# Another order of issue for the 3004 operations of a two-layer decoder trunk

## The chip, the cores and the metric

One core of one Trainium2 chip runs the whole kernel. The time is device microseconds (us) of one execution; the figure for the kernel is the median of its runs. The profile names the engines PE (TensorE, matmuls), PEld (its weight loads, which run beside it), DVE (VectorE), ACT (ScalarE), POOL (GpSimd) and SP (SyncE, which issues most DMA transfers).

## The reference

One sequence of 256 tokens with 1024 channels goes through two layers. Each layer normalises, scales and shifts the input by a vector that a small product with `w_ada` gives, mixes the tokens, and adds the gated result. The even layer has two attention branches (a sliding window with sinks, and a sparse one with compressed, selected and window keys), the odd layer one block-sparse branch with 16 heads of 64.

```python
for layer in range(DEPTH):
    ada = jnp.einsum('bd,de->be', c_act, w_ada[layer]) + b_ada[layer]
    shift, scale, gate = jnp.split(ada, 3, axis=-1)
    h = rms_norm(x, norm_g[layer]) * (1.0 + scale[:, None, :]) + shift[:, None, :]
    ...
    y = even_mixer(...) if layer % 2 == 0 else odd_mixer(h, w_in_odd[i], w_out_odd[i], cos, sin)
    x = x + gate[:, None, :] * y
return rms_norm(x, final_g)

def odd_mixer(h, w_in, w_out, cos, sin):
    proj = jnp.einsum('bsd,de->bse', h, w_in)
    q, k, v, z = jnp.split(proj, _offsets(ODD_SIZES), axis=-1)
    o = moba_attention(q, k, v, cos, sin) * jax.nn.silu(z)
    return jnp.einsum('bse,ed->bsd', o, w_out)
```

## The kernel before

The tokens are two halves of 128 partitions. Weights come in pieces of up to 1 MB into five buffers named `raw`. Full float32 precision is kept by splitting both operands into a high and a low part: ACT casts the high part (`whi`), DVE subtracts it for the low part (`wlo`), and each product is three matmuls, high by high, high by low and low by high (`mm3`; `split`, `load_split` and `split_quad` make the parts). For the activations the parts are called `hhi`, `hlo` and, after the gate path, `ghi`, `glo`. Products land in eight PSUM banks, named `ps_pj`, `ps_s`, `ps_pt`, `ps_o` and `ps_m` by their use.

The vector `ada` is made beside this: `ada_wide` loads pieces of `w_ada` and DVE adds them up, times the condition `cz`, in `acc`; then small matmuls sum `acc` over the partitions (`ada_shift_scale`, `start_sums`, `ada_gate`). The result that scales and shifts the input is `shs`.

Small f32 matmuls use a part of the array each, given by `tile_position`: strips of 32 or 64 rows or columns. `ada_shift_scale` has four column strips, `attn_quad` (attention scores of the odd layer) four row strips, `attn_four` and `attn_values` two strips. Each of these functions hands the list of its matmuls to `plan.group`, which gives all of them the same dependences, so that their order within the group is free but for sums that add up in one place.

What sets the order: the program is written with `Plan`, whose engines record each operation with its dependences in place of issuing it. At the end `issue` issues them all in the order of the list `ORDER` (3004 numbers from line 38 on; number n is the n-th operation recorded). Each engine works through its own instructions in that order, a DMA on the queue of the engine that issues it (nearly all on SP). The names of tiles and buffers were bound while recording, so a list can only reorder: what an operation reads, writes and waits for is fixed. Since every operation is issued by one line, the profile puts nearly all at line 249, and operations are told apart by the names of their tiles.

```python
def issue(self):
    place = {i: n for n, i in enumerate(ORDER)}
    assert len(place) == len(ORDER) == len(self.ops)
    for i in ORDER:
        assert all(place[d] < place[i] for d in self.ops[i]["deps"])
        self.ops[i]["inst"] = self.ops[i]["fn"]()
```

Of the kernel before, what the change touches and what calls it, by code (L numbers as in the profile page):

```python
# [37 lines left out]
0 2 1 4 5 44 9 685 3 10 6 37 88 11 7 38 35 12 87 13 89 14 15 16 86 17 18 85 19 70 90 20 91 21 71 22 92 55 72 23 93 47  # L38
45 24 41 56 25 48 74 57 26 49 94 73 27 28 40 59 58 80 95 42 29 75 50 30 76 104 60 61 62 51 63 77 78 98 65 64 66 67 106
107 108 109 110 111 112 113 114 115 116 52 117 101 79 118 119 120 121 122 123 124 125 126 127 128 129 53 105 130 131  # L40
132 133 134 135 136 137 96 68 97 138 81 145 139 82 31 69 140 83 32 141 100 33 142 147 34 146 99 182 170 149 164 148
183 151 171 143 150 173 84 179 167 102 165 144 158 185 152 186 176 153 103 177 159 178 156 172 154 174 212 200 201 157
213 160 180 184 155 168 162 206 222 36 187 224 194 166 531 175 225 169 195 181 215 188 226 203 189 207 223 202 227 214
228 229 230 231 232 233 234 235 236 161 237 238 239 240 241 242 243 220 244 245 163 246 247 190 248 197 191 198 208
249 204 217 192 257 196 250 209 251 216 259 252 205 199 258 210 274 261 211 253 286 260 283 255 275 295 254 289 530
268 287 262 193 256 277 219 276 290 218 264 296 292 272 288 221 270 284 273 280 269 281 322 266 293 285 334 263 294
324 282 271 278 291 323 297 335 279 307 313 319 267 325 308 314 310 332 301 265 302 336 316 326 304 303 333 337 338
339 340 341 342 343 344 345 346 347 348 349 329 350 351 352 353 354 355 356 357 305 358 320 309 306 311 327 365 312
359 298 367 317 366 328 299 315 330 360 318 361 321 368 362 300 433 363 371 384 369 436 390 402 364 385 393 370 403
405 529 378 391 437 399 396 373 386 331 372 397 374 394 435 380 379 398 420 387 382 438 432 400 376 401 406 404 381  # L50
423 434 388 407 439 389 421 534 408 392 383 411 440 528 395 429 409 687 414 375 424 441 425 430 377 442 443 444 445
446 447 448 449 450 451 452 453 417 454 415 426 455 418 412 413 456 463 422 457 532 459 410 458 416 533 431 464 427
465 682 480 467 419 466 461 492 489 501 460 478 495 481 469 483 468 486 470 476 484 479 502 683 462 482 474 485 428
490 684 471 491 496 475 507 472 497 513 8 504 477 503 505 506 473 493 498 540 499 541 514 932 555 508 509 686 525 557
487 556 519 809 515 537 526 527 558 538 488 500 543 535 494 510 539 607 520 551 516 511 608 542 553 559 517 552 521
536 518 512 554 545 522 549 560 550 546 565 609 566 544 561 934 562 563 617 564 610 571 931 567 572 568 569 690 616
936 573 629 619 620 621 933 611 622 523 570 630 623 577 612 578 574 575 576 618 524 579 583 580 613 581 688 584 585
586 582 638 589 590 631 624 614 632 637 633 625 591 592 626 634 671 627 587 593 689 588 628 595 596 597 598 635 599
600 640 547 641 636 639 642 643 594 548 601 602 644 603 658 604 605 606 659 650 645 646 664 647 651 648 665 652 653
649 654 660 692 655 691 693 694 661 657 662 695 696 656 697 698 663 699 700 666 810 701 702 935 703 670 704 667 668  # L60
705 672 706 707 669 708 938 709 1014 812 710 811 673 674 956 937 742 39 743 43 744 46 745 675 746 813 747 748 749 940
941 942 943 944 945 946 947 957 1021 756 959 960 961 962 963 964 965 966 939 1024 750 948 949 950 951 754 952 953 954
955 751 676 755 958 677 757 967 968 969 970 971 972 973 974 752 1131 678 753 1209 776 679 975 711 54 774 680 1212 712
778 713 714 758 780 715 782 976 759 977 775 978 760 761 979 681 762 716 768 980 864 865 866 779 867 981 868 615 982
874 869 870 781 871 983 872 777 990 984 985 878 986 987 717 783 896 718 880 719 989 764 763 784 720 902 721 722 723
875 988 724 876 725 991 785 1022 769 992 726 787 727 728 993 729 898 765 766 730 900 731 732 786 767 733 734 994 735
1023 1025 736 995 737 738 739 770 771 772 901 996 792 1330 1026 773 1079 1080 1081 740 1082 1083 1084 903 1085 1086
741 873 788 1091 789 793 790 997 814 815 816 791 817 818 1089 897 998 999 1000 1001 1132 1027 819 820 821 822 823 824
1002 825 1109 826 879 827 1133 1003 794 828 829 877 830 831 832 881 1004 795 796 882 833 1111 834 835 836 1005 837 838
839 1115 840 841 842 1093 843 1116 844 845 1087 846 883 847 899 1113 848 849 1006 850 851 885 852 1210 853 854 855 797  # L70
856 857 858 904 859 1090 860 861 1028 1134 905 1135 862 1136 1137 1138 891 1139 1140 906 1141 884 1215 1337 1007 863
798 799 1338 800 907 801 1211 802 909 803 804 1110 805 886 1114 887 888 890 1029 1030 1088 1008 1031 1032 1033 1142
889 1034 914 1035 1036 1331 915 1037 1038 892 893 1143 894 1039 1040 1041 895 1042 1043 908 1044 1009 1045 1332 1046
1047 1112 1048 1049 910 911 1094 1050 1051 1052 1053 1146 1054 1092 1055 1415 1117 912 1010 1056 1057 1058 806 913
1059 1060 1061 1213 1062 1333 1011 1095 1164 1012 1063 1216 1064 916 917 918 1065 1066 1067 1013 919 1068 1096 1334
1069 1070 807 1071 1072 1073 1074 1015 1075 1165 1335 1148 1098 1214 1016 1149 1076 1017 1018 1104 1019 1166 920 921
1020 1414 922 1144 923 1077 924 1168 1411 925 1170 926 1147 927 1410 1118 1078 1267 1145 1268 1269 1270 1097 1120 1339
1099 1126 1100 1101 1217 1218 1150 1171 1219 928 1220 1221 1222 1102 1223 1224 1151 1340 1225 1226 1167 1227 1228 1229
1230 1169 1231 1232 1233 1153 1234 1103 1235 1236 1416 808 1237 929 1238 1239 1240 1407 1241 1172 1105 1275 1242 1436
1243 1125 1406 1244 1245 1152 1246 1279 1247 1248 1119 1249 1250 1173 1158 1434 1106 1107 1437 1251 1252 1253 1254  # L80
1255 1256 1257 1108 1258 1259 1260 1281 1438 1261 1262 1263 1435 1264 1121 1122 1123 1265 1271 1272 1273 1274 1124
1266 1494 1159 1127 1128 1297 1417 1129 1181 1442 1299 1443 1130 1444 1301 1445 1277 1440 1154 1303 1155 1156 1180
1341 930 1342 1157 1343 1344 1175 1174 1441 1160 1161 1278 1162 1446 1447 1163 1454 1455 1280 1439 1176 1177 1298 1178
1456 1457 1179 1458 1459 1351 1276 1182 1504 1355 1183 1300 1184 1408 1345 1185 1346 1347 1348 1302 1186 1304 1187
1371 1188 1375 1189 1282 1353 1190 1373 1191 1192 1193 1349 1374 1194 1305 1283 1195 1306 1196 1284 1197 1409 1356
1198 1199 1352 1200 1201 1202 1286 1203 1285 1204 1431 1307 1292 1205 1412 1287 1314 1430 1288 1289 1448 1449 1354
1450 1350 1451 1206 1452 1308 1453 1460 1357 1290 1291 1461 1358 1413 1534 1462 1293 1294 1295 1463 1464 1296 1465
1535 1491 1566 1207 1542 1309 1490 1310 1311 1466 1313 1543 1377 1312 1544 1545 1359 1360 1418 1315 1316 1317 1467
1546 1318 1472 1567 1372 1336 1361 1362 1366 1363 1419 1319 1376 1320 1321 1378 1322 1323 1536 1324 1325 1379 1326
1365 1505 1380 1327 1208 1328 1495 1364 1420 1421 1422 1423 1329 1382 1381 1367 1432 1368 1424 1369 1547 1473 1370  # L90
1468 1387 1474 1433 1388 1383 1384 1385 1475 1476 1386 1469 1568 1492 1425 1389 1390 1391 1569 1548 1392 1470 1537
1393 1394 1395 1396 1397 1493 1398 1399 1400 1401 1402 1426 1403 1570 1652 1471 1549 1404 1477 1506 1550 1405 1507
1484 1538 1485 1478 1720 1486 1487 1488 1539 1489 1479 1480 1481 1482 1428 1500 1483 1571 1572 1501 1540 1551 1552
1553 1496 1554 1502 1555 1541 1556 1557 1656 1558 1559 1654 1560 1561 1781 1562 1655 1563 1564 1565 1497 1573 1574
1590 1575 1498 1576 1577 1427 1591 1578 1499 1579 1580 1581 1592 1582 1583 1584 1657 1596 1585 1586 1429 1587 1588
# [1272 lines left out]
```

## Time and profile before

| | |
|---|---|
| median of 3 runs | 298.74 us (298.65 to 298.84) |
| the profiled execution, first to last instruction | 296.8 us |
| granted TensorE clock, mean | 0.992 |
| moved by DMA | 71.73 MB, mean 242 GB/s |

The page's table of 40 slices shows what each engine does over the span, a digit for the busy tenths of 7.4 us:

```profile
DVE  0488698799999999999798679799959779999883
ACT  5356246876997899984638863286386338684531
DMA  7999999998992679686886969729828800192003
```

DMA engines are full for about the first 90 us, VectorE nearly full from 60 us on with some gaps, ScalarE and the later DMA half to three quarters used.

### The profile page before, as it was taken

To read this page: it belongs to the slowest core of one execution; us is meant where nothing else is said; L and a number is where in the kernel's file an instruction comes from. 1 tells how busy PE (TensorE), PEld (TensorE's weight loads), DVE (VectorE), ACT (ScalarE), POOL (GpSimd) and SP (SyncE) were. 2 spreads that over 40 slices of the span, in tenths; PEclk is the share of its full clock that TensorE was granted. 3 is DMA by queue.
4 is the path that set the end of the run, shared out by engine and by line. 5 is a ranking of instruction groups with operands and counts; after the bars stand their busy time and mean duration, and the time that the engine had idled before them with its cause. 6 is when DMAs were issued, how large, how long until landed. Compare 5 with 4: busy or idle time off the path is not lost.

```text
span 296.8 us, 6205 instructions
## 1 busy us (share of the span) xinstructions
PE 286.9 (97%) x2297; PEld 246.3 (83%) x2297; DVE 252.2 (85%) x630; ACT 188.5 (63%) x479; POOL 9.2 (3%) x32
## 2 busy tenths in 40 slices
PE   8999999999999999999999999999999989999991
PEld 8778778897788978776768899998899989887891
DVE  0488698799999999999798679799959779999883
ACT  5356246876997899984638863286386338684531
POOL 2100000001000000000020000000000000000021
PEclk9999999999999999999999999999999999999996
DMA  7999999998992679686886969729828800192003
GB/s 242 389 389 377 344 394 372 300 355 240 390 386 71 235 252 352 210 281 212 305 264 190 367 179 301 275 79 311 300 93 280 280 9 2 42 380 75 3 0 141
DMA packets 48479, 71.73 MB, mean 242 GB/s; under 512 B 2522, under 2 KB 33986, under 8 KB 48450
## 3 DMA queue, kind: packets, MB, share of 16 engines
q1 hardware_dynamic: 47906, 70.92, 70.0%
q10 hardware_dynamic: 544, 0.43, 0.4%
q8 instruction: 18, 0.29, 0.4%
q14 instruction: 11, 0.09, 0.1%
HBM read 70.29 MB, written 1.05 MB: 240 GB/s over the span
## 4 chain that ended last, share of the span: by engine, by line
PE 77%; DMA 14%; DVE 4%; ACT 2%; issue 1%; SPq 1%; POOL 1%; DVEq 0%; ACTq 0%
PE ps_pj L249 53%; PE ps_pt L249 7%; PE ps_o L249 6%; PE ps_s L249 6%; PE ps_m L249 5%; DMA raw<-in_w_in_even_dram 5%; DMA qT<-in_w_ada_dram 4%; DMA raw<-in_w_ada_dram 3%; DMA late<-in_w_ada_dram 2%; DVE wlo L249 1%; ACT whi L249 1%; SPq L249 1%; DVE xs L249 1%; DVE t L249 1%; POOL parts L249 1%
## 5 line engine op out<-in xcount | busy, mean ns | idle before, releaser
L249 ACT CAST whi<-raw 128x512 fp32r<-128x512 f32 (+2 forms) x116 | 72.2, 656 | 23.6 <-PE ps_pj L249 18.5
L249 DVE TENSOR_TENSOR wlo<-raw,whi 128x512 fp32r<-128x512 f32 (+2 forms) x100 | 71.8, 741 | 8.9 <-ACT whi L249 8.8
L249 PE MATMUL ps_pj<-hlo,whi 128*128 128x256 f32 x256 | 69.8, 286 | 0.0
L249 PE MATMUL ps_pj<-hhi,wlo 128*128 128x256 f32 x256 | 69.6, 284 | 0.0
L249 PE MATMUL ps_pj<-hhi,whi 128*128 128x256 f32 x256 | 69.5, 286 | 0.0
L249 PEld LDWEIGHTS ps_pj<-hhi,wlo 128*128 128x128 f32 x256 | 47.4, 188 | 1.7 <-issue 1.3
L249 PEld LDWEIGHTS ps_pj<-hhi,whi 128*128 128x128 f32 x256 | 47.0, 188 | 1.1 <-issue 0.3
L249 PEld LDWEIGHTS ps_pj<-hlo,whi 128*128 128x128 f32 x256 | 47.1, 188 | 0.5 <-issue 0.2
L249 DVE SCALAR_TENSOR_TENSOR acc<-raw,cz,acc 128x1024 f32<-128x1024 f32 x24 | 30.7, 1278 | 2.1 <-DMA raw<-in_w_ada_dram 2.0
L249 ACT ACTIVATE late<-late,mn 128x128 f32<-128x128 f32 (+1 forms) x58 | 25.9, 448 | 8.4 <-DVE mn L249 8.4
L249 DVE SCALAR_TENSOR_TENSOR wlo<-raw,whi 128x512 fp32r<-128x512 f32 x32 | 21.4, 686 | 6.3 <-ACT whi L249 6.2
L249 PE MATMUL ps_pj<-whi,hhi 128*128 128x512 f32 (+2 forms) x72 | 25.7, 376 | 0.6 <-ACT hhi L249 0.5
L249 PE MATMUL ps_pj<-whi,hlo 128*128 128x512 f32 (+2 forms) x72 | 26.0, 372 | 0.0
L249 PE MATMUL ps_pj<-wlo,hhi 128*128 128x512 f32 (+2 forms) x72 | 25.6, 367 | 0.0
L249 ACT COPY late<-ps_pt 128x384 f32<-128x384 f32 (+1 forms) x29 | 14.0, 484 | 12.9 <-PE ps_pt L249 12.9
L249 PE MATMUL ps_pj<-whi,ghi 128*128 128x512 f32 (+1 forms) x56 | 20.8, 372 | 0.0
L249 PE MATMUL ps_pj<-wlo,ghi 128*128 128x512 f32 (+1 forms) x56 | 20.5, 366 | 0.0
L249 PE MATMUL ps_pj<-whi,glo 128*128 128x512 f32 (+1 forms) x56 | 20.4, 366 | 0.0
L249 PE MATMUL ps_pt<-ta,late 128*128 128x128 f32 x87 | 16.5, 278 | 0.9 <-DVE late L249 0.9
L249 PEld LDWEIGHTS ps_pj<-whi,hhi 128*128 128x128 f32 x72 | 13.5, 188 | 3.2 <-ACT hhi L249 1.2
L249 ACT ACTIVATE whi<-raw 128x512 fp32r<-128x512 f32 x16 | 10.0, 629 | 9.0 <-PE ps_pj L249 8.7
L249 PEld LDWEIGHTS ps_pj<-whi,hlo 128*128 128x128 f32 x72 | 13.5, 188 | 1.8 <-issue 0.2
(240 smaller groups left out, 589.6 us busy)
## 6 DMA issues: line engine op xcount, KB each, us to landing
raw<-in_w_in_odd_dram SPq DMA_DIRECT2D x16, 1024.0 KB, 5.8
raw<-in_w_ada_dram SPq DMA_DIRECT2D x8, 1024.0 KB, 7.8
raw<-in_w_ada_dram SPq DMA_DIRECT2D x16, 512.0 KB, 6.0
raw<-in_w_in_even_dram SPq DMA_DIRECT2D x5, 1024.0 KB, 9.0
raw<-in_w_in_even_dram SPq DMA_DIRECT2D x7, 652.0 KB, 6.7
late<-in_w_ada_dram SPq DMA_DIRECT2D x16, 256.0 KB, 6.6
raw<-in_w_out_even_dram SPq DMA_DIRECT2D x4, 1024.0 KB, 5.4
raw<-in_w_out_odd_dram SPq DMA_DIRECT2D x4, 1024.0 KB, 9.2
```

The costliest lines, as they stand in the source:

```text
L249: self.ops.append(dict(key=eng.key, deps=deps, fn=lambda: getattr(real, name)(*args, **kw)))
```

## The change

`ORDER` gets another list of the same 3004 numbers. Nothing else differs: operations, tiles, dependences and transfers stay, and each operation stays on its engine. The diff is a block of numbers:

```diff
@@ -35,127 +35,123 @@
-0 2 1 4 5 44 9 685 3 10 6 37 88 11 7 38 35 12 87 13 89 14 15 16 86 17 18 85 19 70 90 20 91 21 71 22 92 55 72 23 93 47
...
-1503 1598 1597 1589 1599 1658 1600 1601 1593 1602 1611 1508 1509 1510 1511 1512 1513 1514 1515 1603 1516 1517 1518
...
+1581 1592 1582 1502 1583 1584 1657 1596 1658 1585 1586 1503 1587 1597 1598 1588 1655 1589 1599 1600 1601 1593 1602 1508
...
```

By engine, the operations that stand at another place in their queue are 1339 of 1912 on PE, 453 of 546 on DVE, 313 of 397 on ACT, 78 of 121 on SP and 17 of 28 on POOL. The first some 10 us and PE's last part, from about 269 us on, keep their order. (The lines of the list are four fewer, so that line 249 is line 245 in the new file.)

Three places show what that means. The rows are an engine's operations in the order of issue: line, operation, output <- inputs with the buffers' numbers, and shape; "x2" means twice in a row.

**The start, DVE at about 36 us.** `raw4` is a piece of `w_in_even`, `wlo` its low part; `shs` is the shift and scale of four channel groups; `oT` and then `hhi`, `hlo` (ACT, DVE) are the scaled input. Before:

```order
L249 SCALAR_TENSOR_TENSOR acc0_106<-qT1_99,cz_72,acc0_106 128x512 x2
L249 TENSOR_TENSOR wlo0_114<-raw4_105,whi0_110 128x512
L249 TENSOR_TENSOR shs_76<-ps_m0_107,rT_73 128x2x2
L249 TENSOR_TENSOR shs_76<-shs_76,rT_73 128x2
L249 TENSOR_TENSOR wlo0_114<-raw4_105,whi0_110 128x512
L249 TENSOR_SCALAR oT_74<-bigA_84,shs_76 128x256
```

and now:

```order
L245 SCALAR_TENSOR_TENSOR acc0_106<-qT1_99,cz_72,acc0_106 128x512
L245 TENSOR_TENSOR shs_76<-ps_m0_107,rT_73 128x2x2
L245 TENSOR_TENSOR shs_76<-shs_76,rT_73 128x2
L245 TENSOR_SCALAR oT_74<-bigA_84,shs_76 128x256
L245 TENSOR_TENSOR wlo0_114<-raw4_105,whi0_110 128x512
L245 TENSOR_SCALAR oT_74<-bigA_84,shs_76 128x256
```

Both splits of `raw4` moved behind `shs`.

**The last load of `w_ada`, SP at about 230 us.** It goes to `raw2`, the last piece but one of the odd layer's input weights to `raw1`. Before:

```order
L249 DMA raw0_101<-in_w_in_odd_dram 128x8x256
L249 DMA raw3_104<-in_w_out_odd_dram 128x4x512
L249 DMA raw1_102<-in_w_in_odd_dram 128x8x256
L249 DMA raw2_103<-in_w_ada_dram 128x2x1024
L249 DMA raw1_102<-in_w_out_odd_dram 128x4x512
```

and now:

```order
L245 DMA raw0_101<-in_w_in_odd_dram 128x8x256
L245 DMA raw3_104<-in_w_out_odd_dram 128x4x512
L245 DMA raw2_103<-in_w_ada_dram 128x2x1024
L245 DMA raw1_102<-in_w_in_odd_dram 128x8x256
L245 DMA gate_77<-in_b_ada_dram 128x1024
```

The two loads changed places. On DVE the product `late_81<-late_81,rc41_149 128x128` that a transpose at 243 us waits for moved from behind the accumulation `acc0_106<-raw2_103,cz_72,acc0_106` to 14 places further ahead.

**A packed group, PE at about 153.6 us.** These are the matmuls of `ada_shift_scale` for the odd layer: five sums of 128 terms on each of four column strips. Before:

```order
L249 MATMUL ps_pj2_96<-ta_63,t40_88 128x128 x4
L249 MATMUL ps_o0_68<-ta_63,t40_88 128x128
L249 MATMUL ps_m0_107<-acc0_106,ones_67 32x256 x4
L249 MATMUL ps_m0_107<-raw4_105,cz_72 32x256 x8
L249 MATMUL ps_m0_107<-raw2_103,cz_72 32x256 x8
```

and now:

```order
L245 MATMUL ps_pj2_96<-ta_63,t40_88 128x128 x4
L245 MATMUL ps_m0_107<-acc0_106,ones_67 32x256
L245 MATMUL ps_m0_107<-raw4_105,cz_72 32x256 x2
L245 MATMUL ps_m0_107<-acc0_106,ones_67 32x256
L245 MATMUL ps_m0_107<-raw4_105,cz_72 32x256
L245 MATMUL ps_m0_107<-acc0_106,ones_67 32x256
L245 MATMUL ps_m0_107<-raw4_105,cz_72 32x256
L245 MATMUL ps_m0_107<-acc0_106,ones_67 32x256
L245 MATMUL ps_m0_107<-raw4_105,cz_72 32x256 x2
L245 MATMUL ps_m0_107<-raw2_103,cz_72 32x256 x2
L245 MATMUL ps_m0_107<-raw4_105,cz_72 32x256 x2
L245 MATMUL ps_m0_107<-raw2_103,cz_72 32x256 x6
```

Before, the strips took turns: 0, 1, 2, 3, 0, 1, 2, 3 and so on. Now their order is 0, 0, 0, 1, 1, 3, 3, 2, 1, 3, 1, 0, 2, 2, 1, 0, 3, 2, 3, 2. The other packed groups are shuffled in the same manner.

235 rows, old and new, of the table ORDER are left out of this document.

## Prediction

> **What bounds the kernel now.** I read the page first, then what TensorE waited for, then the chain that ended last, and then the rows of single stretches.
>
> ```profile
> PE 286.9 (97%) x2297; PEld 246.3 (83%) x2297; DVE 252.2 (85%) x630; ACT 188.5 (63%) x479; POOL 9.2 (3%) x32
> PE 77%; DMA 14%; DVE 4%; ACT 2%; issue 1%; SPq 1%; POOL 1%; DVEq 0%; ACTq 0%
> ```
>
> TensorE (PE) is busy for 97% of the span, and 77% of the chain is its own work. The set of matmuls stays, so the new list can gain only where TensorE stands still, and it can lose where a cover that an operation has now becomes too short. The share of 97% hides small stalls, since a busy PE is not PE at its peak. So I look at the waits.
>
> ```profile
> PE ps_o L249 <- DVE ones L249: 1.1, 1, 1.1
> PE ps_pt L249 <- DVE late L249: 0.9, 1, 0.9
> PE ps_pj L249 <- ACT hhi L249: 0.5, 1, 0.5
> PE ps_pj L249 <- DVE t L249: 0.2, 1, 0.2
> ```
>
> The columns are the total, the number of waits and the longest one. The first row lies at the start of the program, where both lists are the same. The other three are each one place: 243.08, 37.66 and 152.93 us. They are what the change can remove.
>
> **Part 1: the stall at 243 us.**
>
> ```profile
> 241.93 0.27 PE L249 MATMUL ps_pj<-hlo,whi 128*128 128x256 f32 x1
> 243.08 0.30 PE L249 MATMUL ps_pt<-ta,late 128*128 128x128 f32 x1 [0.88 <-DVE late L249]
> ```
>
> These are rows of the timeline (start, duration, what; in brackets the idle time ahead of it and what ended it). Now the chain of waits there, the row of DVE's waits, and the loads of 226 to 241:
>
> ```profile
> 230.22 0.37 SPq L249
> ...
> 230.68 9.33 DMA raw<-in_w_ada_dram
> 240.03 1.28 DVE acc L249
> ...
> 242.74 0.21 DVE late L249
> ...
> 244.09 2.92 PE ps_pj L249 x25
> ...
> DVE acc L249 <- DMA raw<-in_w_ada_dram: 2.0, 1, 2.0
> ...
> raw<-in_w_in_odd_dram SPq DMA_DIRECT2D x1, 1024.0 KB, 5.7
> ```
>
> From the start of one 256-column matmul to the start of the next takes 2.92 / 25 = 0.117 us; here 243.08 - 241.93 = 1.15 us pass, so **1.03 us** are lost. The chain shows how. The load of w_ada was issued at 230.68, behind a load of w_in_odd for which SP had waited until 230.22, and it landed at 240.01. VectorE (DVE) stood still for 2.0 us at the accumulation that reads it (`acc`), with small softmax products (`late`) queued behind it; a transpose needs the one that ended at 242.74 + 0.21 = 242.95.
>
> The new list changes both ends of this. SP issues the w_ada load ahead of the w_in_odd load. So it no longer waits for the buffer of the other load, which came free at 230.2, but only for its own. The w_in_odd load went out at 230.22 and took 5.7 us, to 235.9; in its place w_ada lands at about 236, four us earlier. On DVE, four more operations that do not need it (two splits, two pieces of softmax) now stand ahead of the accumulation, and the `late` product on which the transpose waits stands 14 places earlier, at a place that ran at about 231 us. Either move alone removes the wait. What is late next is the following DVE result, so I take -1.0, with ends -1.03 and 0.
>
> **Part 2: the stalls at 38 and 153 us.**
>
> Rows of the timeline and, from 36.01 on and from 149.13 on, of the chain of waits:
>
> ```profile
> 36.75 0.39 PE L249 MATMUL ps_pj<-whi,hlo 128*128 128x512 f32 x1
> 37.66 0.50 PE L249 MATMUL ps_pj<-whi,hhi 128*128 128x512 f32 x1 [0.53 <-ACT hhi L249]
> ...
> 36.01 0.69 DVE wlo L249
> 36.70 0.08 DVE shs L249
> 37.01 0.61 ACT hhi L249
> ...
> 152.12 0.40 PE L249 MATMUL ps_s<-wlo,ghi 128*128 128x512 f32 x1
> 152.36 0.40 PE L249 MATMUL ps_s<-whi,glo 128*128 128x512 f32 x1
> 152.93 0.66 PE L249 MATMUL ps_pj<-ta,t 128*128 128x128 f32 x4 [0.17 <-DVE t L249]
> ...
> 149.13 0.73 ACT t L249 x2
> 152.38 0.50 DVE t L249
> ...
> 16.94 5.10 DMA late<-in_w_ada_dram
> 22.01 0.86 PE L249 MATMUL ps_m<-late,cz 128*32 128x128 f32 x24
> ```
>
> A 512-column matmul is followed after 152.36 - 152.12 = 0.24 us. At 37.66, 0.91 us pass since the one before: 0.67 lost. The matmul waits for `hhi` (ACT), that for `shs` (DVE), and that stood behind the split `wlo`, which took 36.01 to 36.70 and had itself waited for a load. Now `shs` stands ahead of that split, so `hhi` can come some 0.7 us earlier and the stall goes: -0.67. Against it, at 22.01 the sums over `late` began as soon as their load landed (16.94 + 5.10 = 22.04); in the new list other loads go out ahead of the last `late` loads, and some 0.5 us of new waiting there, a tenth of that load's 5.1, is my estimate. Together **-0.2**, with ends -0.7 and +0.5.
>
> At 152.93, 0.57 - 0.24 = 0.33 us are lost to the norm of one token half: ACT (sum of squares), two POOL operations, DVE `t`. The addition on DVE that feeds the ACT step at 149.13 now stands three places earlier, and the ACT step three places earlier too, ahead of two casts. So the chain starts earlier by more than 0.33: **-0.3**, with ends -0.33 and 0.
>
> **Part 3: the order inside packed groups.** Small f32 matmuls that use a strip of the array (32 or 64 rows or columns) stand in groups; all operations of a group wait for the same things. Before, neighbours in a group use different strips (2 same-strip neighbours in the program, 316 on different strips). In the new list they are shuffled: 79 same-strip neighbours, 239 others.
>
> ```profile
> 79.03 0.43 PE L249 MATMUL ps_m<-hg,w2k 128*64 128x32 f32 x8
> 79.39 0.38 PE L249 MATMUL ps_pj<-hlo,whi 128*128 128x256 f32 x1
> 79.02:79.06 0.04, 0.03 (x2) 0.03 (x2) 0.04 (x1) 0.04 (x2) 0.00 (x0) 1.00 0.97 307
> 79.09:79.13 0.04, 0.04 (x4) 0.04 (x4) 0.04 (x1) 0.04 (x2) 0.00 (x0) 1.00 2.63 871
> ...
> 153.62 0.64 PE L249 MATMUL ps_m<-acc,ones 128*32 128x256 f32 x8
> 154.08 1.91 PE L249 MATMUL ps_m<-raw,cz 128*32 128x256 f32 x32
> 155.92 0.33 PE L249 MATMUL ps_o<-ta,t 128*128 128x128 f32 x1
> ```
>
> Each f32 matmul has two records, its two passes. At 153.62 stand 20 matmuls, 40 passes, 155.92 - 153.62 = 2.30 us: ten passes on each of four strips, so 0.23 us for a pass of 256 columns and four abreast. The two passes of one matmul stand next to each other in the program and need the same strip. If passes never overtook each other, a strip's second pass would hold up all others, at most two would run abreast, and this group would take 20 x 0.22 = 4.4 us. So TensorE looks past a busy strip. How far? At 79.03 the program has two matmuls on one strip, then two on the other: eight passes. They took 0.36 us. The first two start within 0.04 us, the next two by 0.07 later (the x2 and x4 of PE in two stretches of the window view). At 0.36 / 8 us or more a pass, one strip can't start two so close, so the second strip began with three passes of the first still pending.
>
> If it looks farther than the new order needs, the price is only that of strips that run out early at a group's end: **+0.4** over some 25 groups. If it looks no farther than those four passes of a strip, a group stalls where a fifth comes too early. The group of 153.62 now begins with three matmuls on one strip: four passes, 0.9 us; a group of 20 at 121.8 the same, one at 268.0 0.4, four score groups (190, 206, 237 and 255 us) 0.2 each, two others 0.2 each: **+3.4**. I take +0.4, because no row shows a limit, and keep 0 and 3.4 as ends.
>
> The Trainium skill bears on this in two places that differ. "TensorE: Matmul & The Clock Gate", under The mechanism of its Part 3, says that matmuls start and end strictly in program order; "TensorEngine Tiling (Array Packing)", Key Properties, says that tiles run independently. By the first the shuffled groups would cost over 10 us, an estimate with every same-strip neighbour holding up the array for a pass of 0.1 to 0.22; the group at 153.62 speaks against it with 2.30 us where 4.4 would follow, so as a rival it gets no chance here.
>
> **Part 4: transposes.** They are spread among the matmuls more finely than before (263 changes of kind in place of 193).
>
> ```profile
> 247.01 0.11 PE ps_pt L249
> 249.58 0.33 PE ps_pt L249 x3
> ```
>
> One alone takes 0.11, three in a row 0.33: no price to be seen. I take +0.1, ends 0 and +0.4.
>
> **Sum.** -1.0 - 0.2 - 0.3 + 0.4 + 0.1 = -1.0 us. The profiled execution's span is 296.8, and the median of the runs is 298.74, so 1.9 lie around the span. 295.8 + 1.9 = **297.7 us**. The tail after the last matmul (290.4 to 296.8) keeps its chain: only operations off it trade places.
>
> **Rivals.** *A: short look-ahead (slower).* One mechanism, in the packed groups: +3.4 in place of +0.4 gives 300.7. It decides as soon as TensorE holds no more than four passes of a strip; with six, by counting the new order, the price is back at 0.4. For it: nothing shows more than four. Against it: nothing shows a bound either.
>
> *B: DVE becomes the bound, and the gain is given back.*
>
> ```profile
> 240.00:245.00 5.00, 4.12 (x36) 3.95 (x36) 4.96 (x18) 2.94 (x10) 0.00 (x0) 1.00 0.00 0
> 245.00:250.00 5.00, 5.00 (x46) 5.00 (x45) 5.00 (x16) 4.41 (x16) 0.00 (x0) 1.00 0.01 3
> 250.00:255.00 5.00, 4.96 (x45) 4.38 (x45) 4.91 (x10) 3.79 (x7) 0.00 (x0) 1.00 0.00 0
> ```
>
> The columns after the stretch's length are PE, PEld, DVE and ACT busy. DVE is full from 240 to 255. If TensorE arrives there 1.0 earlier and DVE does not, the wait comes back at 251 or later, and similar new waits can come up wherever 453 moved DVE operations were only just in time: without the 1.0 the sum is 0, 298.7; with another 0.5 to 1.0 of such waits up to 299.7. Against it: DVE itself gains the 2.0 us that it stood still.
>
> *C: everything fits.* No price in the groups and none at 22 us: -1.0 - 0.7 - 0.3 = -2.0, 296.7.
>
> *D: the change does not do what it says at 243*: the w_ada load is still late, since the load ahead of it in the queue is as large. 298.7, like B.
>
> **How the numbers follow.** Forecast with its own range 297.1 to 298.3: 0.38. C: 0.14. B and D: 0.28, half of it within 0.2% and the rest above. A: 0.20. A measurement can tell about 0.2%, 0.6 us, from no change. Faster (under 298.14): 0.33 of the forecast's 0.38 and all of C, and 0.02 of A mixed with gains of C: 0.49. Within: 0.05 + 0.14 + 0.04 of A with C = 0.23. Slower: 0.14 of A and 0.14 of B: 0.28. The range from 296.5 to 300.7 leaves out the far half of A and a little beyond C.
>
> **What would show it.** Right: no DVE wait for in_w_ada in the stretch around 236 to 243, no TensorE wait for `late` there, `hhi` no longer ending a wait at 38, the group at 153 still at about 2.3 us and the score groups at 1.5. Wrong: those groups at 3.1 and 1.7 us (A), or a new wait row of TensorE for DVE after 250 us (B). A new wait for a load would be a case that I have left out: transfers traded places at some 40 places, and I found cover for those that I followed.

## The result and the profile after

| | before | after |
|---|---|---|
| median of the runs | 298.79 us (298.65 to 299.16, 4 runs) | 301.12 us (300.82 to 301.61, 4 runs) |
| ratio, 95% interval | | 1.0073 [1.0055, 1.0091] |
| profiled execution, first to last instruction | 296.8 us | 299.9 us |

The change makes the kernel slower, by 2.3 us between the medians and 0.73% by the ratio, just above the range of the prediction. The profiled executions lie 3.1 us apart, since that of after is the slowest of its four; the account below is of these 3.1 us. The page of after, in the lines shown for before:

```profile
PE 290.9 (97%) x2297; PEld 250.9 (84%) x2297; DVE 253.9 (85%) x630; ACT 188.2 (63%) x479; POOL 8.3 (3%) x32
PE 89%; DMA 7%; issue 1%; ACT 0%; DVE 0%; SPq 0%; POOLq 0%; POOL 0%; ACTq 0%
```

TensorE is busy for 4.0 us more (290.9 against 286.9) with the same 2297 records, and its share of the chain has grown from 77% to 89%. So the time was not lost in waiting for others. The waits of TensorE confirm it:

```profile
PE ps_o L245 <- DVE ones L245: 1.1, 1, 1.1
PE ps_pj L245 <- ACT whi L245: 0.4, 1, 0.4
PE ps_m L245 <- DMA late<-in_w_ada_dram: 0.4, 1, 0.4
PE ps_pj L245 <- ACT t L245: 0.3, 1, 0.3
```

The rows for `late` (243 us), `hhi` (38 us) and DVE `t` (153 us, where a shorter wait is left) are gone. Two new ones lie at 20 and 24 us, and the last is at 8 us. The stalls are gone, and yet the kernel is slower: matmuls themselves take longer. The timeline of PE in after shows where, at the packed group that was at 153.62 before:

```profile
154.07 0.40 PE L245 MATMUL ps_s<-whi,glo 128*128 128x512 f32 x1
154.46 0.66 PE L245 MATMUL ps_pj<-ta,t 128*128 128x128 f32 x4
155.04 0.62 PE L245 MATMUL ps_m<-acc,ones 128*32 128x256 f32 x2
155.50 0.38 PE L245 MATMUL ps_m<-raw,cz 128*32 128x256 f32 x1
155.50 0.43 PE L245 MATMUL ps_m<-acc,ones 128*32 128x256 f32 x3
155.71 0.38 PE L245 MATMUL ps_m<-raw,cz 128*32 128x256 f32 x1
155.74 0.41 PE L245 MATMUL ps_m<-acc,ones 128*32 128x256 f32 x3
155.93 2.39 PE L245 MATMUL ps_m<-raw,cz 128*32 128x256 f32 x30
158.25 0.44 PE L245 MATMUL ps_o<-ta,t 128*128 128x128 f32 x2
```

From the start of the group to the next operation it takes 158.25 - 155.04 = 3.21 us where it took 2.30. Nothing is waited for inside. The first rows show how: in the 0.46 us before the next row begins, the group's first row holds two passes (x2), where before it held eight. A pass is one of the two records that each of these f32 matmuls leaves.

The place where time is lost can be read by comparing the start of the same matmul in both traces, at points up to which both lists have issued the same set of TensorE operations (after minus before):

| at (before, us) | lag, us | between |
|---|---|---|
| 59.3 | +0.4 | new waits at 20 and 24, none at 38 |
| 106.8 | +0.1 | |
| 121.8 | +0.4 | |
| 125.2 | +1.3 | packed group of 20 |
| 152.9 | +1.5 | two packed groups of 10 |
| 156.1 | +2.4 | packed group of 20 |
| 189.1 | +2.5 | |
| 213.5 | +3.2 | two score groups |
| 239.4 | +3.6 | score group |
| 244.8 | +2.6 | the stall at 243 is gone |
| 252.7 | +2.3 | the one at 251 is gone |
| 269.5 | +3.4 | score group, value group |
| end | +3.1 | |

The whole loss stands in the packed groups, 24 of which can be compared from 69 us on: 37.9 us before (start of the group to start of the next operation), 42.1 after, +4.2. All the rest together gains 1.1 (two more groups, at 117 and 121 us, are mixed with each other in the new list and count with the rest).

### The profile page after: what moved, and what is told of

Read it like the earlier page. It is cut to its first block, busy times and chain, and to the rows that moved or that the text cites. A ratio compares the mean times of both kernels' runs of the same rounds, so it can differ in the third digit from the quotient of the medians.

```text
span 299.9 us, 6183 instructions
## 1 busy us (share of the span) xinstructions
PE 290.9 (97%) x2297; PEld 250.9 (84%) x2297; DVE 253.9 (85%) x630; ACT 188.2 (63%) x479; POOL 8.3 (3%) x32
## 4 chain that ended last, share of the span: by engine, by line
PE 89%; DMA 7%; issue 1%; ACT 0%; DVE 0%; SPq 0%; POOLq 0%; POOL 0%; ACTq 0%
PE ps_pj L245 58%; PE ps_s L245 9%; PE ps_o L245 8%; PE ps_pt L245 7%; PE ps_m L245 6%; DMA late<-in_w_ada_dram 4%; DMA qT<-in_w_ada_dram 2%; DMA xs<-in_x_dram 1%; ACT t L245 0%; SPq L245 0%; DVE t L245 0%; POOLq L1359 0%; DVE xs L245 0%; POOL parts L245 0%; ACTq L245 0%
## 5 line engine op out<-in xcount | busy, mean ns | idle before, releaser
L245 ACT CAST whi<-raw 128x512 fp32r<-128x512 f32 (+2 forms) x116 | 71.3, 657 | 31.4 <-PE ps_pj L245 15.7
L245 PE MATMUL ps_pt<-ta,late 128*128 128x128 f32 x87 | 18.9, 274 | 0.0
L245 PEld LDWEIGHTS ps_pj<-wlo,hhi 128*128 128x128 f32 x72 | 13.2, 188 | 2.2 <-issue 0.3
```

Source lines behind the costliest of these rows:

```text
L245: self.ops.append(dict(key=eng.key, deps=deps, fn=lambda: getattr(real, name)(*args, **kw)))
```

## The experiments

Every experiment is another list, most of them built from one of the two by moving few numbers; the diffs show the part of the list that tells it. The runs of before beside them are those of the same chip.

**e1: after, packed groups in turns again.** In 29 of the 30 groups the matmuls were put back into the order in which the strips take turns, in the places that the new list gives the group.

```diff
-1503 1587 1597 1598 1588 1655 1589 1599 1600 1601 1593 1602 1508
-1512 1516 1509 1513 1511 1603 1515 1510 1594 1517 1519 1521 1520
...
+1503 1587 1597 1598 1588 1655 1589 1599 1600 1601 1593 1602 1508
+1509 1510 1511 1512 1513 1603 1514 1515 1594 1516 1517 1518 1519
```

> The new list, with the matmuls of 29 of the 30 packed groups put back into the order in which the strips take turns (each group keeps its places in the program; nothing else changes). Theory S, short look-ahead (four passes of one strip at most may stand at TensorE, a fifth holds up all that follows): the groups lose the 4.0 us that the two traces show between them (43.8 before, 47.7 after), all but 0.1, so 301.1 - 3.9 = 297.2 us, and the group at about 155 us takes 2.3 us again. Theory L, the shuffled groups are only where some waiting shows that another operation causes: the waiting turns up elsewhere, 300.5 or more.

Measured: 297.12 us, ratio to before 0.9921 [0.9893, 0.9950]. The timeline of PE:

```profile
153.24 0.64 PE L245 MATMUL ps_m<-acc,ones 128*32 128x256 f32 x8
153.70 1.91 PE L245 MATMUL ps_m<-raw,cz 128*32 128x256 f32 x32
155.54 0.44 PE L245 MATMUL ps_o<-ta,t 128*128 128x128 f32 x2
```

The group takes 155.54 - 153.24 = 2.30 us again, and the 24 groups together 37.7. By this alone the median falls by 4.0 us (4.5 if each list is held against the runs of before beside it), and the groups by 4.4. The kernel is now faster than before by 2.2: the new list's other moves together are good, and the shuffling cost more than they brought. Theory L falls.

**e2: before, with only the groups shuffled.**

```diff
-1503 1598 1597 1589 1599 1658 1600 1601 1593 1602 1611 1508 1509 1510 1511 1512 1513 1514 1515 1603 1516 1517 1518
...
+1512 1516 1509 1513 1511 1515 1510 1603 1517 1519 1521 1520 1594 1514 1518 1525 1524 1604 1523 1522 1527 1526 1595 1653
```

> The list of before, with only the matmuls inside 28 packed groups put into the new list's order. S: +3.3 us by counting fifth passes, up to +3.8 by the measured groups, so 302.1 to 302.6 us; the group at 153.6 takes 3.2 us, the score groups 1.85. L: within 0.5 us of before, 298.8 to 299.3.

Measured: 302.68 us against 299.32, ratio 1.0107 [1.0080, 1.0135], +3.4 us in the medians. The timeline of PE around 153 us:

```profile
154.06 0.40 PE L245 MATMUL ps_s<-whi,glo 128*128 128x512 f32 x1
154.44 0.66 PE L245 MATMUL ps_pj<-ta,t 128*128 128x128 f32 x4
...
155.14 0.62 PE L245 MATMUL ps_m<-acc,ones 128*32 128x256 f32 x2
...
158.35 0.44 PE L245 MATMUL ps_o<-ta,t 128*128 128x128 f32 x2
```

The group takes 158.35 - 155.14 = 3.21 us, and the score groups take 1.84 to 1.95: each has the same duration as in after, though all around it is the old order. So in these runs a group's duration follows its own order, whatever stands around it.

**e3 and e4: two and three of a strip in a row.** How far does TensorE look past a busy strip? Both start from before; e3's group at 153 reads as the first line, e4's as the second (1508 to 1527 go over the strips in turns, so 1508, 1512, 1516 are three of strip 0):

```diff
+1508 1512 1509 1513 1510 1514 1511 1515 1603 1516 1520 1517 1521 1594 1518 1522 1519 1523 1604 1524 1525 1526 1527
...
+1508 1512 1516 1509 1513 1517 1510 1514 1603 1518 1511 1515 1519 1594 1520 1524 1521 1525 1604 1522 1526 1523 1527
```

> The list of before, with 26 packed groups ordered so that two matmuls of a strip stand in a row, then two of the next strip (0,0,1,1,2,2,3,3,...): four passes of one strip in a row, never five before the others had their turn. S with a limit of four passes for each strip: +0.2 us, 299.0. Theory W, a window over the passes of the whole program, of about eight passes: +5 us, 304, since the third strip's first pass is the ninth. A limit of three passes for each strip: +6 us, 305.

> The same with three matmuls of a strip in a row in 25 groups: six passes of one strip in a row. S with four passes: two passes too many at each change of strip, +8.6 us by counting, 307.4. With a limit of five: +4.3, 303.1. With six or more: +0.4, 299.2. W with eight passes: +5, 304.

Measured: e3 299.91 us, ratio 1.0020 [1.0001, 1.0039]; e4 307.43 us, ratio 1.0267 [1.0235, 1.0298], against 299.32. The group at 153, e3's three rows first, then e4's:

```profile
154.12 0.66 PE L245 MATMUL ps_m<-acc,ones 128*32 128x256 f32 x8
154.58 1.95 PE L245 MATMUL ps_m<-raw,cz 128*32 128x256 f32 x32
156.46 0.44 PE L245 MATMUL ps_o<-ta,t 128*128 128x128 f32 x2
```

```profile
156.50 0.62 PE L245 MATMUL ps_m<-acc,ones 128*32 128x256 f32 x2
156.96 0.38 PE L245 MATMUL ps_m<-raw,cz 128*32 128x256 f32 x1
156.97 0.40 PE L245 MATMUL ps_m<-acc,ones 128*32 128x256 f32 x1
157.18 0.38 PE L245 MATMUL ps_m<-raw,cz 128*32 128x256 f32 x1
...
158.31 1.92 PE L245 MATMUL ps_m<-raw,cz 128*32 128x256 f32 x22
160.17 0.44 PE L245 MATMUL ps_o<-ta,t 128*128 128x128 f32 x2
```

Two matmuls (four passes) of a strip in a row cost this group 156.46 - 154.12 - 2.30 = 0.04 us; its first row again holds eight passes. Three (six passes) cost 160.17 - 156.50 - 2.30 = 1.37, and the first row has two. A stretch that begins 0.1 us behind the group's start shows how many strips run by then (e3, then e4; the columns are those of the prediction's window views, PE first):

```profile
154.20:154.30 0.10, 0.10 (x4) 0.10 (x8) 0.10 (x1) 0.00 (x0) 0.00 (x0) 1.00 0.84 266
156.60:156.70 0.10, 0.10 (x1) 0.04 (x2) 0.10 (x1) 0.00 (x0) 0.00 (x0) 1.00 0.52 164
```

e3 rules out a window of about eight passes over the whole program: the third strip's first pass is the ninth there, and yet all four strips run at once. It also rules out a limit of three for each strip, and e4 one of five or more: there the second strip starts at 156.97, when two of the first strip's six passes are done and its third begins (156.96). What is left is **four passes of one strip**; a fifth stops all that follows it until a pass of that strip is done. Whether TensorE counts passes or f32 matmuls (two passes each) these runs do not tell, since all packed matmuls here leave two. Some groups in the four orders, in us from the start of the group to the next operation:

| group (time in before) | before | e3: two | e4: three | after |
|---|---|---|---|---|
| 153.6, 20 on four column strips | 2.30 | 2.33 | 3.66 | 3.21 |
| 121.8, 20 on two column strips | 3.61 | 3.67 | 4.10 | 4.59 |
| 237.5, 16 on four row strips | 1.52 | 1.64 | 2.50 | 1.85 |
| 268.0, 8 on two column strips | 1.45 | 1.50 | 1.93 | 1.93 |

The prediction's count for rival A was right in size: for after it gave 0.9, 0.9, 0.2 and 0.4 for these rows, measured are 0.91, 0.97, 0.33 and 0.48. Row strips cost more than counted: e4's group at 237.5 takes 0.97 more, where three changes of strip with two passes of some 0.11 us each give 0.66. Two in a row are not quite free there either (0.12 us a group), and e3's 0.6 in the medians is more than the 0.2 that was expected. The reason stays open.

That e4's median came out as counted is partly luck. All its groups from 69 us on take 10.4 us more than in before, not 8.6, and the median rises by 8.1. Part of what a longer group costs is taken out of later waits: in e4 the transpose at 243 us no longer waits, though DVE still stands 2.2 us for the load.

**e5 and e6: the stall at 243 us, one number each.** e5 takes the last load of `w_ada` (2797) ahead of the `w_in_odd` load (2669); e6 takes the softmax product (2200) 14 places ahead on DVE and leaves the load.

```diff
-... 2188 2613 2452 2669 2453 2610 2454 2455 2456 2393 2797 2394
+... 2188 2613 2452 2797 2669 2453 2610 2454 2455 2456 2393 2394
```

```diff
-2454 2455 2456 2393 2797 2394 2194 2457 2458 2549 2459 2460
+2454 2455 2456 2393 2797 2394 2194 2457 2458 2200 2549 2459 2460
```

> The list of before with one number moved: the last load of w_ada goes out ahead of the w_in_odd load that stood before it. If the stall at 243 us comes from that load alone: it lands near 236 instead of 240, DVE's wait of 2.0 us for it goes and so does TensorE's 1.03, -1.0 us against before. Rival D, the queue of transfers is as long either way: w_ada lands after 239 and less than 0.3 us is gained.

> The list of before with one number moved: the softmax product that the transpose at 243 us waits for stands 14 places earlier on DVE; the load stays late. If that product alone holds TensorE up: DVE still waits 2.0 us for the load, but TensorE loses nothing at 243, -1.0 us. Rival B: the other DVE results behind the accumulation are as late, TensorE waits for the next of them, and -0.3 us or less is left.

Measured, against 299.12: e5 296.97 us, ratio 0.9932 [0.9908, 0.9956]; e6 298.92, ratio 0.9989 [0.9969, 1.0009]. Of e5 a row of TensorE's waits, the load among those of 226 to 241, and PE around 243 us:

```profile
PE ps_m L245 <- DMA gate<-in_w_ada_dram: 0.7, 1, 0.7
...
raw<-in_w_ada_dram SPq DMA_DIRECT2D x1, 1024.0 KB, 5.6
...
242.62 0.28 PE L245 MATMUL ps_pj<-hlo,whi 128*128 128x256 f32 x1
242.74 0.27 PE L245 MATMUL ps_pt<-ta,late 128*128 128x128 f32 x1
```

The load takes 5.6 us in place of 9.33, and the transpose follows its predecessor after 0.12 us in place of 1.15. Of e6 the row of DVE's waits and PE around 252 us:

```profile
DVE acc L245 <- DMA raw<-in_w_ada_dram: 2.3, 1, 2.3
...
251.11 0.28 PE L245 MATMUL ps_pj<-hlo,whi 128*128 128x256 f32 x1
252.02 0.39 PE L245 MATMUL ps_pj<-hhi,whi 128*128 128x256 f32 x1 [0.63 <-DVE t L245]
```

In e6 the transpose at 243 doesn't wait either, but DVE still stands for 2.3 us, and TensorE pays at 252.02: 0.91 - 0.12 = 0.79 us for a rotation (`t`) that DVE reaches too late. So both theories have their half: moving the load brings the gain, and moving the product alone only moves the wait (rival B). e5's gain in the medians is 2.2 us (1.3 to 2.8 by the interval). Its trace shows 1.0 at 243 and 0.3 more at 251, the low end of that; the rest is not explained. The profiled span is only 0.7 shorter than that of before: this execution is the slowest of its seven and lost 0.9 by 38 us, where the two lists are the same (the 0.7 us of the first row above lie there).

**e7: the stall at 38 us alone.** The cast and the split of `raw4` (365, 366) go behind `shs` (360, 361) and `hhi` (362).

```diff
-... 327 365 312 359 298 367 317 366 328 299 315 330 360 318 361 321 368 362 300 433 363 371
+... 327 312 359 298 367 317 328 299 315 330 360 318 361 321 368 362 365 300 433 363 366 371
```

> The list of before with four numbers' order changed at 36 us: on DVE the two small shs operations ahead of the split of raw4, on ACT the scaled input hhi ahead of that piece's cast. If the stall at 38 us is worth its length: -0.67 us. Rival: the transfers bind this stage, so that what is gained at 38 is lost at the next load or split: within 0.2 us of before.

Measured: 298.90 us against 299.12, ratio 0.9986 [0.9961, 1.0011]. PE in e7, and behind it the same matmul in before:

```profile
36.51 0.40 PE L245 MATMUL ps_pj<-whi,hlo 128*128 128x512 f32 x1
36.74 0.39 PE L245 MATMUL ps_pj<-whi,hhi 128*128 128x512 f32 x1
...
43.22 0.34 PE L245 MATMUL ps_o<-wlo,hhi 128*128 128x408 f32 x1
44.05 0.45 PE L245 MATMUL ps_o<-whi,hlo 128*128 128x408 f32 x1 [0.49 <-DVE hlo L245]
```

```profile
44.06 0.34 PE L249 MATMUL ps_o<-wlo,hhi 128*128 128x408 f32 x1
44.26 0.46 PE L249 MATMUL ps_o<-whi,hlo 128*128 128x408 f32 x1
```

The wait at 38 is gone: the matmul starts at 36.74 in place of 37.66, 0.92 earlier. Seven us later 0.83 pass between two matmuls where before 0.20 did, for the low part `hlo` that DVE makes behind further splits and sums, and only 0.21 is left. The rival is right that the gain is lost again at once, but the traces show DVE and not a transfer in the way: it works without a wait from 37.0 us on and begins that `hlo` at 43.58, against 43.78 in before.

**e9: the first 59 us in the new order, the rest in the old.**

> The operations of the first 59 us in the new list's order, all others in the old order (packed groups of the start hold no fifth passes, so they cost nothing). My step for the start was -0.2 us; the two traces stand 0.4 apart at 59 us the other way: new waits for late and raw loads at 20 and 24 us, about 1.1, against 0.7 saved at 38 us. If that is the order's doing: +0.4 us against before, with TensorE waits for ACT whi and for the late load. If it is only the transfers' varying from run to run: within 0.2 us and no such waits.

Measured: 299.89 us against 299.10, ratio 1.0016 [0.9997, 1.0035]. The waits of TensorE in e9:

```profile
PE ps_m L244 <- DMA late<-in_w_ada_dram: 0.4, 1, 0.4
PE ps_pj L244 <- ACT whi L244: 0.4, 1, 0.4
```

Both waits come with the order, and its trace is 0.76 behind before's at 59 us. By 68 us it is 1.7 behind, with two short waits for DVE `t` at 67 and 68 us that neither full list has, so this run also pays for the seam between the two orders. The time is not clear of no change, so the size of the start's loss stays open between 0 and 1 us.

**e8: the better of the two orders by stretches, groups in turns.** The list is that of e7 up to 59 us, the new one from there to 107 us, and so on as the expectation says; over a thousand numbers differ from before, so no diff is shown.

> A list put together by stretches: the old order (with the change at 36 us) up to 59 us and in 107 to 122, 156 to 235 and 253 to 277, the new one elsewhere, with all packed groups in turns. By the differences between the traces stretch by stretch: -0.67, -0.55 (59 to 107), -0.3 (122 to 156), -1.3 (235 to 253), -0.2 (after 277), in all -3.0 us against before, 296.0. If the gains hang on what the new list does elsewhere (transfers above all): no better than the 297.1 of the new list with its groups in turns.

Measured: 297.06 us against 299.12, ratio 0.9941 [0.9919, 0.9962]. The 296.0 that was added up by stretches was not reached. Its profiled span is 294.7, the shortest of all, but its median is no better than e1's and e5's, as the expectation's second case had it. Their intervals overlap, so which of the three is best is open; all three are faster than both kernels.

## Why the prediction was wrong

The step that failed is in Part 3, "I take +0.4, because no row shows a limit". There is a limit, of four passes for each strip, and that rival A put into numbers: +3.4 us for the groups and 300.7 in all. Measured are +4.2 in the groups and 301.1. The rows that I had, eight passes on two strips at 79 us, showed four passes of a strip standing at TensorE and not more; e3 and e4 show that it ends there. The evidence reached exactly as far as the limit, and I took what lay beyond it to be free.

That the other terms come out near their sum is partly luck: -1.4 was forecast for them, and all but the groups gains 1.1 in the traces. The start's wrong sign (+0.4) is made up by 0.3 each between 59 and 107 us and at 251 us, which no term of the sum had.

Point by point:

- Part 1, -1.0 at 243: right in size, -1.0 by the lag table and 1.03 in e5 (1.15 - 0.12). "Either move alone removes the wait" was wrong in what it is worth: the load alone does (e5), the product alone hands the wait on to 252 us (e6).
- Part 2, -0.2 for the start: wrong sign, +0.4 in the traces at 59 us. New waits there were priced at 0.5 and come to 0.8 in after, half of them for a `raw` load that the step had not named. The other half, -0.67 at 38, went, but it is worth 0.2 at 44 us and nothing that the runs can tell (e7).
- Part 2, -0.3 at 153: the wait shrank from 0.34 to 0.16, since 154.46 - 154.07 = 0.39 us pass there now, against 0.57 before. The DVE operation on which it hangs still ends last. That its chain was moved ahead is not shown to be the reason: e2, with the old order there, has 154.44 - 154.06 = 0.38 too.
- Part 3: above. That passes overtake each other was right: without it the group of 153 would take 4.4 us by the prediction's own estimate, and it takes 3.21 even when shuffled.
- Part 4, +0.1 for the transposes: not measured alone. e1 has them about as finely spread as after and is 2.2 faster than before, so what they cost, if anything, is less than the other moves bring.
- Rival B in its first form, that DVE gives the gain at 243 back: not in after or e5, since there DVE no longer waits for the load; it is what happens in e6.

## What to carry to other kernels

Where small f32 matmuls share the array, let the strips take turns in the program, or put at most two f32 matmuls (four passes) of a strip in a row. Two in a row in 26 groups cost 0.6 us here (0 to 1.2 by the interval); three made the groups of the table 14 to 64% longer. A search that moves operations must know this, since to dependences and durations all orders within a group look the same. And a bound that the evidence just reaches is a bound to be priced, not to be assumed away.

## What the runs showed of the hardware

TensorE's look-ahead past a busy strip is counted for each strip, not over the program: with four passes of each of four strips in a row all four start together (2.33 us for 40 passes of 256 columns, 2.30 in turns), and with six they do not (3.66). So on TensorE the order of issue is not the order of start across strips: in e3 the first strip's second matmul (154.58) stands ahead of the other strips' first ones, and yet starts behind them (all within the first row, from 154.12 on).

The first 40 us vary from run to run: e5's list is the old one there, yet its profiled execution is 0.89 us late at 37.66, after a wait of 0.7 for a load. Medians of several runs are needed for any change of less than 1 us.
